# Down projection of a SwiGLU layer: float32r pairs made at each use, and scaled float16 pairs split once and kept in DRAM

## The chip, the cores and the metric

The kernel runs on one NeuronCore of a Trainium2 chip. TensorE (PE in the profile) multiplies, VectorE (DVE), ScalarE (ACT) and GpSimd (POOL) do the elementwise work, and SyncE (SP) issues nearly all transfers, in order, from one queue to 16 DMA engines. The metric is the device time of one execution in microseconds; of several runs the median is given.

## The reference

One layer of a hybrid backbone: 128 context tokens and 1024 latent tokens (1152 in all, nine blocks of 128), width 1024. A modulated RMS norm is followed by one input projection, which feeds a grouped-query attention (8 query heads, 2 key/value heads) and a bidirectional mLSTM (4 heads), side by side; an output projection merges them. Then comes the part that the change touches, the SwiGLU feed-forward layer with D_FF = 2816:

```python
def swiglu(h, w_gu, w_down):
    g, u = jnp.split(h @ w_gu, 2, axis=-1)
    return (jax.nn.silu(g) * u) @ w_down

    x = x + g1 * mix
    h2 = rmsnorm(x, norm2_w) * (1 + sc2) + sh2
    x = x + g2 * swiglu(h2, w_gu, w_down)
```

All inputs and outputs are float32. w_down has 2816 x 1024 elements: 22 row tiles of 128 rows.

## The kernel before

**Pairs.** No product is made in plain float32. A factor is split in a high part and the rest, and a product is the sum of three: high by high, high by rest, rest by high. In the input projection both parts are float16: the weights of a head are brought to a common power of two (class `Scaled`, L180: an absolute sum on ACT, four small DVE operations in `powers`, L159, a transpose and a one-row product in `power_scale`, L167), then split (`pairs`, L209). In the output projection and the feed-forward layer both parts are float32r: `load_piece` (L139) loads 512 KB of raw weights, ACT casts them (L152), and POOL, or DVE for each third piece, subtracts (L135). It has two raw buffers and five of each part. Each weight is loaded and split anew for each chunk.

**Chunks.** The feed-forward layer works on three chunks of three blocks (384 tokens). For a chunk, `gate_up` (L1275) makes, for a row tile f of 128 of the 2816 features, gate and up products of 24 matmuls each (384 columns), then tanh on ACT (L1298), two DVE operations (L1299, L1300) to the tile `tn`, and the pair `hl` by ACT (L1303) and POOL (L135). `down` (L1307) multiplies a group's rows by w_down, for each half of 512 output columns and each of the three blocks, through `three_blocks` (L1082; products L1090 to L1092), first block 0, then blocks 1 and 2. `add_gated` (L1076) multiplies the sum in PSUM by the gate row and adds it to x1. A group is 4 or 5 row tiles, five groups a chunk: gate/up of a group, then down of it, then the next. The last group of the last chunk has its own function, `down_last` (L1334; products L1356 to L1358), which finishes block by block and stores.

**Order.** The program is written as generators that yield after each unit of PE work. `weave` (L62) advances a side generator in proportion to the main one, `emit` runs one to its end; a scheduler then orders each engine's instructions by a simulated timeline, with the order of writing as priority (`hot` raises it). Beside the feed-forward work of a chunk runs the attention of the next chunk (50 units); then `attn_out` (L1178) merges it, and `norm2` (L1223) of the next chunk runs beside the last group's down projection. `finish` (L1319) normalises and stores the chunk before.

**The mLSTM stage.** `head_project` (L717) projects one head; beside it runs the scan of the head before (`head_mlstm`, L764) and, beside heads 0 to 2, `ada_rest` (L437), which loads the modulation weights (L443, three buffers, two loads ahead) and multiplies them (L318). The tiles b0 to b2 of the pool `hp` lie idle until attention.

**Banks.** In the feed-forward part PSUM has four banks of the kind `mm`, shared by gate/up, down, output projection and transposes; attention's scores and values have their own.

## Time and profile before

| | |
|---|---|
| median of 3 runs | 1627.77 us (1623.84 to 1633.02) |
| profiled execution, span | 1626.0 us (its time is given as the span alone) |
| mean granted TensorE clock | 0.972 |
| PE busy | 1517.4 us, 93% |
| DVE, ACT, POOL busy | 970.8, 732.5, 606.5 us |
| moved by DMA | 232.73 MB |

A line of the profile that groups instructions reads: line of the code, engine, operation, out<-in by the names of tiles, shapes, count | busy us in all, mean ns of one | idle us of the engine just before them, and what ended that idle time. A line of a table by stretches has the stretch, its length, then for PE, PE's weight loads, DVE, ACT and POOL the busy time and the count, the granted clock, the busy share of the DMA engines and GB/s. A line of the timeline has start, duration, engine, line and operation; matmuls are pipelined, so the distance between two starts, not the duration, tells the rate. A line of waits has who waited for whom, us in all, times, longest; a line of one tile's instructions has the count, then least, median and most ns.

### The profile page before, as it was taken

The page shows a single profiled execution, that of the slowest core. Times are in us where ns is not written, and L with a number is a line of the kernel's source. Part 1 is how long each engine was busy: PE and PEld are TensorE (multiplying, and loading weights), DVE is VectorE, ACT ScalarE, POOL GpSimd, SP SyncE. Part 2 cuts the span into 40 slices and gives each one's busy share as a digit, 9 for nine tenths or more (in the row PEclk, how much of TensorE's full clock was granted, in tenths as well). Part 3 has the DMA queues.
Part 4 walks back from the last instruction along what each step waited for, and adds up shares of the span by engine and source line. Part 5 has one row for each costly group of instructions (what it writes and reads, how often), then busy time and mean ns, then how long its engine had stood idle before and what let it go on. Part 6 is the DMA issues. An engine that isn't in the chain of part 4 may idle for free. (4 is left out here: it accounts for less than half of the span.)

```text
span 1626.0 us, 23528 instructions
## 1 busy us (share of the span) xinstructions
PE 1517.4 (93%) x8688; PEld 1258.8 (77%) x8688; DVE 970.8 (60%) x2059; ACT 732.5 (45%) x1251; POOL 606.5 (37%) x387
## 2 busy tenths in 40 slices
PE   5899899899879768999999999999999999999996
PEld 2745566575557557998989899898898989899995
DVE  3843364958987665467672646777674474432445
ACT  3744252434544554545643344565562453333332
POOL 0411020404344514443435354444344444545443
PEclk8999999999999878999999999999999999999998
DMA  9355352201156855767873546777684445545441
GB/s 357 94 165 130 101 147 58 84 21 46 41 198 147 195 107 112 168 168 174 187 184 112 149 141 219 187 184 173 156 183 128 134 142 170 152 126 149 130 142 66
DMA packets 386313, 232.73 MB, mean 143 GB/s; under 512 B 169910, under 2 KB 346502, under 8 KB 386198
## 3 DMA queue, kind: packets, MB, share of 16 engines
q1 hardware_dynamic: 384342, 228.04, 52.7%
q10 hardware_dynamic: 1856, 3.19, 0.6%
q8 instruction: 68, 1.11, 0.3%
q14 instruction: 47, 0.39, 0.1%
HBM read 181.16 MB, written 11.69 MB: 119 GB/s over the span
## 5 line engine op out<-in xcount | busy, mean ns | idle before, releaser
L135 POOL TENSOR_TENSOR wlo<-raw,whi 128x1024 fp32r<-128x1024 f32 x146 | 357.8, 2454 | 445.7 <-ACT whi L152 407.9
L152 ACT CAST whi<-raw 128x1024 fp32r<-128x1024 f32 x219 | 224.4, 1025 | 375.9 <-DMA raw<-in_w_gu_dram 137.8
L1272 PE MATMUL mm<-aTl,whi 128*128 128x384 f32 (+2 forms) x1088 | 364.7, 335 | 0.7 <-POOL aTl L135 0.7
L1273 PE MATMUL mm<-aTh,wlo 128*128 128x384 f32 (+2 forms) x1088 | 364.4, 335 | 0.0
L1271 PE MATMUL mm<-aTh,whi 128*128 128x384 f32 (+2 forms) x1088 | 363.4, 336 | 0.7 <-DVE tn L1299 0.7
L1272 PEld LDWEIGHTS mm<-aTl,whi 128*128 128x128 f32 x1088 | 205.9, 189 | 1.7 <-POOL aTl L135 0.9
L1271 PEld LDWEIGHTS mm<-aTh,whi 128*128 128x128 f32 x1088 | 205.4, 189 | 2.0 <-DVE tn L1299 1.3
L1273 PEld LDWEIGHTS mm<-aTh,wlo 128*128 128x128 f32 x1088 | 205.8, 189 | 0.1
L135 DVE TENSOR_TENSOR wlo<-raw,whi 128x1024 fp32r<-128x1024 f32 (+1 forms) x73 | 88.1, 1206 | 142.2 <-ACT whi L152 141.7
L1090 PE MATMUL mm<-whi,hl 128*128 128x512 f32 x372 | 145.8, 397 | 1.5 <-ACT hl L1303 1.4
L1091 PE MATMUL mm<-wlo,hl 128*128 128x512 f32 x372 | 146.9, 397 | 0.0
L1092 PE MATMUL mm<-whi,hl 128*128 128x512 f32 x372 | 144.3, 396 | 0.7 <-POOL hl L135 0.7
L1007 DVE SCALAR_TENSOR_TENSOR pl<-pr,st,ph 128x1152 f16<-128x1152 f32 (+1 forms) x72 | 107.8, 1498 | 39.4 <-ACT ph L1006 39.4
L488 PE MATMUL wi<-ipair,hT 128*128 128x384 f16 (+2 forms) x392 | 128.2, 327 | 2.8 <-ACT ipair L216 2.8
L489 PE MATMUL wi<-ipair,hT 128*128 128x384 f16 (+2 forms) x392 | 128.1, 327 | 0.0
L490 PE MATMUL wi<-ipair,hT 128*128 128x384 f16 (+2 forms) x392 | 127.1, 326 | 0.0
L135 POOL TENSOR_TENSOR hl<-tn,hl 128x384 fp32r<-128x384 f32 x66 | 84.2, 1276 | 105.0 <-ACT hl L1303 105.0
L1003 ACT ACTIVATE pr<-S,st 128x1152 f32<-128x1152 f32 (+1 forms) x72 | 81.1, 1127 | 89.1 <-DVE st L1002 86.1
L1299 DVE SCALAR_TENSOR_TENSOR tn<-tn,mm 128x384 f32<-128x384 f32 (+2 forms) x68 | 36.7, 540 | 137.9 <-PE mm L1273 97.5
L1080 DVE TENSOR_TENSOR x<-x,t 128x512 f32<-128x512 f32 x102 | 116.5, 1163 | 0.8
L1000 PE MATMUL S<-kst,qT 128*128 128x384 f32 (+1 forms) x400 | 88.3, 355 | 19.6 <-ACT pr L1003 19.2
L1002 DVE TENSOR_REDUCE st<-S 128x1 f32<-128x1152 f32 (+1 forms) x72 | 88.9, 1234 | 18.3 <-PE S L1000 17.8
(353 smaller groups left out, 2684.6 us busy)
## 6 DMA issues: line engine op xcount, KB each, us to landing
raw<-in_w_gu_dram SPq DMA_DIRECT2D x132, 512.0 KB
raw<-in_w_down_dram SPq DMA_DIRECT2D x60, 512.0 KB
a<-in_w_ada_dram SPq DMA_DIRECT2D x32, 512.0 KB
gl<-g_d SPq DMA_DIRECT2D x36, 256.0 KB
aw<-in_w_ada_dram SPq DMA_DIRECT2D x16, 512.0 KB
iraw<-in_w_in_dram SPq DMA_DIRECT2D x32, 256.0 KB
raw<-in_w_out_dram SPq DMA_DIRECT2D x15, 512.0 KB
x<-in_x_sample_dram SPq DMA_DIRECT2D x13, 512.0 KB
```

The source lines that it names most:

```text
L135: (dve if eng == "dve" else pool).tensor_tensor(out=out, in0=full, in1=hi, op=ALU.subtract)
L152: nc.scalar.copy(hi[:, :n], raw[:, :n])
L488: mm(ps[:, :n], ah, wh[:, k % 2, c0 : c0 + n], start=(k == 0), stop=False)
L489: mm(ps[:, :n], ah, wl[:, k % 2, c0 : c0 + n], start=False, stop=False)
L490: mm(ps[:, :n], al, wh[:, k % 2, c0 : c0 + n], start=False, stop=(k == KD - 1))
L1080: eng.tensor_tensor(out=x1[:, cs], in0=x1[:, cs], in1=t, op=ALU.add)
L1090: mm(ps, ah, wh[:, k % 2, :], start=(k == 0), stop=False)
L1091: mm(ps, ah, wl[:, k % 2, :], start=False, stop=False)
L1092: mm(ps, al, wh[:, k % 2, :], start=False, stop=(k == nk - 1))
L1271: mm(ps, wh[:, k, :], th[:, k, :], start=(k == 0), stop=False)
L1272: mm(ps, wh[:, k, :], tl[:, k, :], start=False, stop=False)
L1273: mm(ps, wl[:, k, :], th[:, k, :], start=False, stop=(k == KD - 1))
```

## The change

w_down is split once. `split_down`, run beside the projections of heads 0 and 1, takes each of the 22 row tiles: load 512 KB, an absolute sum per row on ACT, `powers` on DVE to get a power of two for each row, a scaled copy in float16 on ACT, the rest in float16 on DVE, and a store of the pair (512 KB) to a DRAM tile. The row scales stay in `wds`.

The down projection then loads float16 pairs straight into a ring of three tiles `wd` (each two row tiles by 512 columns, 512 KB), with no cast. The activations `tn` of a group are kept as float32, each with an absolute sum; when the group is whole, `rescale` finds one power of two for it (a maximum on DVE, a transpose, a maximum, `powers`, a one-row product, two small DVE operations), and each `tn` becomes a float16 pair with the row scale of w_down folded in (ACT, DVE). `tn` and pairs share 13 slots. `add_gated` undoes the scale.

Groups become 10 and 12 row tiles (10, 8 and 4 in the last chunk). Down of a group no longer follows its gate/up: it runs after the first four products of the next group; a chunk's last group is rescaled beside the first units of `attn_out` and multiplied after it, beside `norm2`. A half of the down projection now fills the three blocks' banks at once. `one1` and `wds` move to a pool that stays, and a scratch space of the program is made smaller.

```diff
-GROUPS = [(0, 4), (4, 4), (8, 4), (12, 5), (17, 5)]
-LAST = [(0, 5), (5, 5), (10, 4), (14, 4), (18, 4)]
+GROUPS = [(0, 10), (10, 12)]
+LAST = [(0, 10), (10, 8), (18, 4)]
+SLOTS = 13
...
+    wd_d = [drp.tile([P, 2, 2, 2, 512], F16, name=f"wd_d{j}") for j in range(NF // 2)]
...
+    def split_down():
+        def load(f):
+            t = hp.tile([P, 3, 1024], F32, name=nm("wdt"), tag=f"b{f % 3}")
+            dma(t[:, 0], w_down[f * P : (f + 1) * P, :])
+            return t
+        ahead = [load(0), load(1)]
+        yield
+        for f in range(NF):
+            t = ahead.pop(0)
+            if f + 2 < NF:
+                ahead.append(load(f + 2))
+            raw, v = t[:, 0], wds[:, f, :]
+            act(t[:, 2].bitcast(BF16)[:, 0:1024], raw, AF.Abs, accum_out=v[:, 0:1])
+            powers(v, P)
+            yield
+            o = t[:, 1].bitcast(F16).rearrange("p (n h x) -> p n h x", n=2, h=2)
+            raw = raw.rearrange("p (n x) -> p n x", n=2)
+            act(o[:, :, 0], raw, AF.Copy, scale=v[:, 2:3])
+            dve.scalar_tensor_tensor(out=o[:, :, 1], in0=raw, scalar=v[:, 2:3], in1=o[:, :, 0], op0=ALU.mult, op1=ALU.subtract)
+            dma(wd_d[f // 2][:, :, f % 2], o)
+            yield
...
-    weave(head_project(0, sts[0]), beside((gates, 0.6), (ada, 0.45)), 56, 56)
+    weave(head_project(0, sts[0]), beside((gates, 0.6), (ada, 0.45), (wd_steps, 0.4)), 56, 56)
...
-    weave(head_project(1, sts[1]), beside((scan, 1.15), (ada, 0.45)), 56, 56)
+    weave(head_project(1, sts[1]), beside((scan, 1.15), (ada, 0.45), (wd_steps, 0.45)), 56, 56)
+    emit(wd_steps)
...
-            hl = hlp.tile([P, 2, CT], F32R, name=nm("hl"), tag="hl", bufs=5)
-            ah, al = hl[:, 0], hl[:, 1]
-            nc.scalar.copy(ah, tn)
-            sub(al, tn, ah.bitcast(F32), "pool")
-            acts.append((ah, al))
+            jk = ft.tile([P, D], BF16, name=nm("jk"), tag="t2", bufs=3)
+            act(jk[:, 0:CT], tn, AF.Abs, scale=wds[:, f, 3:4], accum_out=g["st"][:, i : i + 1])
+            g["a"].append(tn)
+
+    def rescale(g):
+        f0, nf = g["f0"], g["nf"]
+        m = fp.tile([P, 16], F32, name=nm("gm"), tag="gm", bufs=2)
+        v = fp.tile([1, 4], F32, name=nm("gv"), tag="gv", bufs=2)
+        with hot(200):
+            dve.tensor_reduce(out=m[:, 0:1], in_=g["st"][:, 0:nf], axis=AX.X, op=ALU.max)
+            ps = bank()
+            transpose(ps[0:1, 0:P], m[:, 0:1])
+            dve.tensor_reduce(out=v[:, 0:1], in_=ps[0:1, 0:P], axis=AX.X, op=ALU.max)
+            powers(v, 1)
+        yield
+        with hot(200):
+            ps = bank()
+            mm(ps[:, 0:2], one1, v[:, 2:4], start=True, stop=True)
+            dve.tensor_copy(m[:, 1:3], ps[:, 0:2])
+            dve.tensor_scalar(out=m[:, 4 : 4 + nf], in0=wds[:, f0 : f0 + nf, 3], scalar1=m[:, 1:2], scalar2=None, op0=ALU.mult)
+        g["inv"] = m[:, 2:3]
+        for i, tn in enumerate(g["a"]):
+            hl = hlp.tile([P, 2, CT], F16, name=nm("hl"), tag="hl", bufs=SLOTS)
+            sc = m[:, 4 + i : 5 + i]
+            act(hl[:, 0], tn, AF.Copy, scale=sc)
+            dve.scalar_tensor_tensor(out=hl[:, 1], in0=tn, scalar=sc, in1=hl[:, 0], op0=ALU.mult, op1=ALU.subtract)
+            g["hl"].append(hl)
+        yield
...
+    def down_rows(g, j, n, tag="wd", bufs=3):
+        w = wp.tile([P, 2, 2, 512], F16, name=nm("wd"), tag=tag, bufs=bufs)
+        dma(w, wd_d[(g["f0"] + j) // 2][:, n])
+        return w
+
+    def down(c, a, g):
+        for n in range(2):
+            gate = gate_bc(1, c, n)
+            banks = [bank() for _ in range(CB)]
+            for j in range(0, g["nf"], 2):
+                w = down_rows(g, j, n)
+                for i, ps in enumerate(banks):
+                    down_products(ps, g, j, i, w)
+                    if j + 2 == g["nf"]:
+                        add_gated(a["x1"][i], ps, gate(c * CB + i), n, inv=g["inv"])
+                    yield 2
...
+    def groups(c, a, grps):
+        held = None
+        for g in grps:
+            ups = gate_up(a, g, 0, g["nf"])
+            if held is not None:
+                r = rescale(held)
+                next(r)
+                yield next(ups)
+                emit(r)
+                if g["nf"] > 4:
+                    for _ in range(3):
+                        yield next(ups)
+                    yield from down(c, a, held)
+                    yield from ups
...
-            emit(groups(c, cur, GROUPS[NG:-1]))
-            f0, nf = GROUPS[-1]
-            emit(gate_up(cur, f0, nf))
+            r = rescale(grps[-1])
+            next(r)
+            ao = attn_out(c + 1, nxt, oT, out_gates())
+            for _ in range(3):
+                next(ao)
+            emit(r)
+            emit(ao)
             n2 = chain(*[norm2(c + 1, nxt, i) for i in range(CB)])
-            weave(chain(down(c, cur, f0, nf, 0), down(c, cur, f0, nf, 1)), n2, 6 * nf, 8)
+            weave(down(c, cur, grps[-1]), n2, 6 * GROUPS[-1][1], 8)
```

`down_products` makes the same three products of a row tile and a block as L1090 to L1092, with float16 factors; `down_last` uses it with the tiles that `down_rows` loads.

112 lines of the change are left out of this document (49 added, 63 removed).

## The prediction

> **What bounds the kernel now.** I read first the page's shares, then stretches of the span in a table of busy time, then the waits of TensorE, and last the spacing of single matmuls in the timeline.
>
> ```profile
> PE 1517.4 (93%) x8688; PEld 1258.8 (77%) x8688; DVE 970.8 (60%) x2059; ACT 732.5 (45%) x1251; POOL 606.5 (37%) x387
> ```
> ```profile
> core 0: us, PE busy (x) PEld busy (x) DVE busy (x) ACT busy (x) POOL busy (x), PEclk, DMA share, GB/s
> 0.00:20.00 20.00, 13.12 (x69) 4.91 (x71) 5.78 (x29) 3.12 (x5) 0.76 (x6) 1.00 0.92 350
> ...
> 80.00:165.00 85.00, 82.10 (x554) 44.76 (x552) 35.14 (x115) 35.72 (x71) 9.72 (x12) 1.00 0.55 148
> 165.00:255.00 90.00, 87.50 (x632) 59.02 (x633) 43.41 (x154) 34.04 (x99) 13.15 (x21) 0.98 0.47 124
> ...
> 640.00:960.00 320.00, 315.50 (x1782) 290.60 (x1781) 181.42 (x262) 152.69 (x202) 135.97 (x66) 0.99 0.64 159
> 960.00:1310.00 350.00, 346.10 (x1916) 315.98 (x1915) 228.43 (x329) 175.55 (x233) 149.30 (x70) 1.00 0.65 168
> 1310.00:1606.00 296.00, 294.17 (x1544) 272.14 (x1543) 131.22 (x181) 101.28 (x134) 139.79 (x70) 1.00 0.47 139
> ```
>
> The last three rows are the feed-forward part, one row for each chunk of three blocks. TensorE (PE) stands idle there for 4.5 + 3.9 + 1.8 = 10.2 us of 966, at a granted clock of 0.99 to 1.00; DVE, ACT and POOL are at most 65%, 50% and 47% busy. So only what shortens TensorE's own stream, or those 10.2 us, can move the end there. The two rows from 80 to 255 are the first two mLSTM heads, where the change puts new work.
>
> A busy PE is not PE at its peak, so I take the rate from starts in unbroken runs: the down projection now (24 matmuls), the same width in float16 in the query projection (26), and a gate/up run (46).
>
> ```profile
> 1607.45 0.40 PE L1356 MATMUL mm<-whi,hl 128*128 128x512 f32 x1
> ...
> 1612.80 0.40 PE L1358 MATMUL mm<-whi,hl 128*128 128x512 f32 x1
> ```
> ```profile
> 445.79 0.38 PE L488 MATMUL mm<-ipair,hT 128*128 128x512 f16 x1
> ...
> 451.19 0.38 PE L490 MATMUL mm<-ipair,hT 128*128 128x512 f16 x1
> ```
> ```profile
> 860.10 0.34 PE L1271 MATMUL mm<-aTh,whi 128*128 128x384 f32 x1
> ...
> 867.90 0.34 PE L1271 MATMUL mm<-aTh,whi 128*128 128x384 f32 x1
> ```
>
> 5.35 us / 23 = 232.6 ns for one f32 matmul of 512 columns, 5.40 / 25 = 216.0 ns for one in f16, 7.80 / 45 = 173.3 ns in gate/up. The middle run has what the change makes: a pair of f16 halves on each side, three products, 512 columns.
>
> **Part 1, the product type.** The down projection has 396 triples:
>
> ```profile
> L1091 PE MATMUL mm<-wlo,hl 128*128 128x512 f32 x372 | 146.9, 397 | 0.0
> ...
> L1357 PE MATMUL mm<-wlo,hl 128*128 128x512 f32 x24 | 9.5, 394 | 0.0
> ```
>
> (372 + 24) x 3 = 1188 matmuls, before and after, each 16.6 ns closer to the next: **-19.7 us**, all on PE's own stream. 24 of these triples lie in the tail, where DVE finishes; they are 1.2 us of it.
>
> The Trainium skill, TensorE: Matmul & The Clock Gate, Back-to-back issue gap, gives one warm gap, N / 2.4 + 2.5 ns, that does not ask for the type: 215.8 ns at 512 columns. The f16 run agrees, the f32 run at 232.6 does not. By that rule the term would be zero; it is a rival below.
>
> **Part 2, work taken off the other engines.** The 60 full loads of raw w_down (and, by the code, 12 half ones) stay as 66 loads of pairs of 512 KB, the same bytes, but each loses its cast and its subtraction.
>
> ```profile
> raw<-in_w_down_dram SPq DMA_DIRECT2D x60, 512.0 KB
> ```
> ```profile
> L135 POOL TENSOR_TENSOR wlo<-raw,whi 128x1024 fp32r<-128x1024 f32 x132 | 330.9, 2511 | 413.0 <-ACT whi L152 375.2 <-issue 10.8 <-DVE t L1079 8.4
> L152 ACT CAST whi<-raw 128x1024 fp32r<-128x1024 f32 x195 | 204.5, 1049 | 326.3 <-DMA raw<-in_w_gu_dram 127.4 <-PE mm L1272 58.4 <-DMA raw<-in_w_down_dram 48.1
> ...
> L1080 DVE TENSOR_TENSOR x<-x,t 128x512 f32<-128x512 f32 x97 | 110.8, 1165 | 0.8
> L135 POOL TENSOR_TENSOR hl<-tn,hl 128x384 fp32r<-128x384 f32 x66 | 84.2, 1276 | 105.0 <-ACT hl L1303 105.0
> ...
> L1079 DVE TENSOR_TENSOR t<-mm,gl 128x512 f32<-128x512 f32 x88 | 58.5, 684 | 36.1 <-PE mm L1092 17.6 <-DMA gl<-g_d 10.4 <-PE mm L1358 6.7
> ...
> L1300 DVE TENSOR_TENSOR tn<-tn,mm 128x384 f32<-128x384 f32 x64 | 35.4, 553 | 1.6
> ...
> L1303 ACT CAST hl<-tn 128x384 fp32r<-128x384 f32 x66 | 33.7, 510 | 34.2 <-DVE tn L1300 34.0
> ```
>
> POOL loses the activations' subtraction (84.2) and, two pieces of three, some 40 x 2.5 us: about 185 us. ACT loses 60 x 1.049 us of casts and the half ones, 63 and a little, and gains 66 absolute sums, by the cast of a tile of that size (L1303) and a read of the accumulator (Part 4) 0.51 + 0.19 each: 46 us. DVE loses 48 of 90 gated additions, because 7 groups take the place of 15, at 0.684 + 1.165 us: 89 us; and gains the 66 activation subtractions, by L1300 about 37 us. PE covers all of it now and the sum takes **nothing** for it; without the cover it would be worth at most the 10.2 idle us.
>
> **Part 3, group boundaries.** PE's waits over these 966 us:
>
> ```profile
> PE S L1000 <- ACT pr L1003: 2.9, 2, 1.6
> PE mm L1090 <- ACT hl L1303: 1.4, 2, 1.1
> ...
> PE mm L1092 <- POOL hl L135: 0.7, 2, 0.5
> ```
>
> Waits for hl are of the old kind: projection, then at once the products that need its last row. Running a group's down products after four products of the next group takes these away, and a lighter DVE some of the others. Bounds 0 and -10.2; I take **-4**, nearer to the named waits (with their share of the pipeline's refill) than to the whole.
>
> The new rescale is late next. Its chain after a group's last row: ACT sum 0.51 + 0.19, eight small DVE operations of about 0.162, two small PE operations, then an ACT copy 0.51 and a DVE subtraction 0.55; queued behind its waits are, on PE, a transpose and a one-row product, and the whole down projection of the group.
>
> ```profile
> L1004 DVE RECIPROCAL st<-st 128x1 f32<-128x1 f32 x45 | 7.3, 162 | 41.8 <-ACT pr L1003 41.7
> ```
> ```profile
> L176 PE MATMUL mm<-pv,one 1*128 1x2 f32 x12 | 2.5, 273 | 1.7 <-DVE pv L165 1.7
> ...
> L114 PE MATMUL mm<-ident,isc 128*1 128x128 f32 x6 | 1.7, 289 | 4.5 <-DVE rv L125 4.5
> ```
>
> That is 0.70 + 1.30 + 0.56 + 1.06 = 3.6 us and its hand-overs. Between groups the cover is 4 x 24 x 0.1733 = 16.6 us; at the ends of the first two chunks it is the first output-projection block, 24 x 0.2326 = 5.6 us, and thin. If uncovered there: 7.2 us. PE's own 14 small operations cost between nothing and 7 x 0.56 = 3.9 us. Together 0 to 11; I take **+4**: half of the small operations, and a slip of 1 us at each thin place.
>
> Two more edits with the answer nothing. A group of twelve has one of the 13 activation slots to spare, so each pair waits for the tile before it to be given up: 1.06 us a row, while PE spends 9 x 0.216 = 1.9 us on it. And a down half now holds three of the four PSUM banks: the next half's first two blocks (12 x 0.216 = 2.6 us) start in the spare bank and in the one that was finished first, which covers an evacuation by DVE (0.684); uncovered, 12 halves would cost 8 us, and the range holds that.
>
> **Part 4, the split, 80 to 255 us.** For each of 22 row tiles: a load and a store of 512 KB, an absolute sum and a scaled copy on ACT, four small operations and a subtraction on DVE. The input weights go through the same operations in that stretch:
>
> ```profile
> L199 ACT ACTIVATE jk<-iraw x13: 1041/1057/1057, 87.9 to 307.0; 128x1024 bf16<-128x1024 f32 x13
> L199 ACT ACTIVATION_READ_ACCUMULATOR jk<-iraw x13: 185/186/188, 88.9 to 308.0; 128x1 f32 x13
> ...
> L216 ACT ACTIVATE ipair<-iraw,isc x8: 1146/1148/1165, 81.8 to 303.5; 128x1024 f16<-128x1024 f32 x8
> ...
> L217 DVE SCALAR_TENSOR_TENSOR ipair<-iraw,isc,ipair x8: 1272/1283/3143, 83.0 to 308.4; 128x1024 f16<-128x1024 f32 x8
> ```
>
> ACT: 22 x (1.057 + 0.186 + 1.148) = 52.6 us into 105 idle. DVE: 22 x (1.283 + 4 x 0.162) = 42.5 into 96 idle. The DMA engines: 23.1 MB, at the 350 GB/s of the first 20 us 66 us, onto 0.55 x 85 + 0.47 x 90 = 89 busy: 155 of 175. PE hides it while its stream never waits for a late a or ipair. SP runs its queue in order, and the 44 new issues (with a load that waits for an earlier store to land) stand among these:
>
> ```profile
> SPq L443 <- PE mm L318: 73.2, 20, 16.2
> ```
> ```profile
> PE mm L318 <- DMA a<-in_w_ada_dram: 4.4, 1, 4.4
> ```
>
> From 0 (all hidden, as nearly all loads are now) to 22 (five more such waits of 4.4): I take **+4**, one more.
>
> **Sum.** -19.7 - 4 + 4 + 4 = -15.7. The profiled execution's span is 1626.0, and no other time is given for it; so 1610.3. The median of the runs, 1627.77, stands 1.8 above that span: **1612 us**.
>
> **The rivals.** 0.5% is 8 us, about what a measurement of this kernel tells from no change.
>
> More: the boundary waits go entirely and split and rescale hide: -19.7 - 10.2 = -29.9, **1598**. For it: DVE and POOL much lighter. Against it: most of the 10.2 is attention's.
>
> No rate gain, f16 weights in the down stream still spaced at 232.6: -4 + 4 + 4, **1632**. Against it: the f16 run above, at 512 columns. This is what the Trainium skill's rule in Part 1 would come to.
>
> The split isn't hidden: ada's and the head weights' loads come late, five waits of 4.4: -19.7 - 4 + 4 + 22, **1630**. For it: DMA at 155 of 175, SP waits up to 16.2 us. Against it: one such wait now.
>
> Slower: the ring of three weight tiles. Before, five hi/lo slots lay between landing and use; now PE reads the landed tile itself, and its slot is refilled only after its 18 matmuls. A tile lasts 18 x 0.216 = 3.9 us, so two ahead cover 7.8. Landings on the chain of waits:
>
> ```profile
> 1352.81 6.72 DMA raw<-in_w_gu_dram
> ...
> 1365.53 5.80 DMA raw<-in_w_down_dram
> ...
> 1379.23 4.59 DMA raw<-in_w_down_dram
> ```
>
> These and about 0.4 of issue fit. Beyond 7.8 us a tile takes (latency + 3.9) / 3. There are 62 tiles on this path (22 + 22 + 18); the result is slower by 0.5% from (15.7 + 8.1) / 62 = 0.38 us a tile, so from a mean latency near 9 us. At 9.5 it is 4.47 a tile, +35: **1647**. For it: SP's order and attention's transposes. Against it: nothing landed that late here.
>
> **Chances.** Forecast 0.58 (own range 1602 to 1619), more 0.12, no rate gain 0.06, split not hidden 0.11, ring 0.13. Faster: forecast and more, 0.70. Same: 0.06 + 0.11 = 0.17. Slower 0.13. Range: down to 1598 less 3 for the spread of runs, 1595; up through 1630 and 1632 to 1633, which leaves out the ring.
>
> **What would show it.** Right: the down products at 216 ns from start to start, x396 for each of the three; PE's idle time from 640 to the end at or below 10 us; no PE wait on the wd tiles; 80 to 255 not longer by more than 5 us. Wrong: PE waits on DMA wd or on hl above 1 us each group (ring, rescale), a later first gate/up product than now (split), or a spacing near 232 ns.

## The result, and where the time went

The change makes the kernel slower. Its median is 1671.43 us (1668.08 to 1672.53, 4 runs) against 1625.80 us of the kernel before on the same chip (1617.71 to 1633.02, 4 runs): a ratio of 1.0278, with a 95 % interval from 1.0236 to 1.0320, some 45 us. The forecast was 1612 us, with a range up to 1633.

The profiled execution of the changed kernel has a span of 1669.1 us (its time is 1670.91), 43.1 us more than the span before. The page's shares:

```profile
PE 1526.5 (91%) x8709; PEld 1170.8 (70%) x8709; DVE 943.3 (57%) x2171; ACT 756.7 (45%) x1377; POOL 404.7 (24%) x273
```

POOL lost a third of its work, as forecast, and PE is busy 9 us longer although its products are quicker. The first gate/up product divides the span in two. A row of one line's instructions has the count, least, median and most ns, and then the first and the last start in us; first the kernel before, then the changed one:

```profile
L1271 PE MATMUL mm<-aTh,whi x70: 220/281/455, 622.1 to 667.0; 128*128 128x256 f32 x32, 128*128 128x128 f32 x32, 128*128 128x384 f32 x6
```
```profile
L1286 PE MATMUL mm<-aTh,whi x32: 279/283/364, 647.0 to 666.1; 128*128 128x256 f32 x32
```

Ahead of it 24.9 us are lost (622.1 to 647.0), behind it 18.2 (1003.9 to 1022.1), where the forecast had some 4 and -20. These are single traces: three later kernels that leave the feed-forward part as it was (`split_only`, `split_work`, `split_transfers`, below) took 999.5 to 1000.7 us behind the first product, so a difference of a few us between two traces says little.

**Ahead of it: the split.** The table by stretches of the changed kernel, with a stretch that the prediction did not look at (40 to 80 us, the preparation of the inputs); after it the row of the kernel before for that stretch:

```profile
core 0: us, PE busy (x) PEld busy (x) DVE busy (x) ACT busy (x) POOL busy (x), PEclk, DMA share, GB/s
40.00:80.00 40.00, 29.55 (x196) 21.91 (x196) 35.58 (x122) 34.82 (x74) 15.54 (x13) 0.84 0.73 234
80.00:165.00 85.00, 76.19 (x513) 41.75 (x511) 54.74 (x182) 58.72 (x104) 15.20 (x19) 0.98 0.87 281
165.00:255.00 90.00, 83.06 (x576) 54.46 (x575) 45.96 (x155) 45.90 (x112) 8.96 (x20) 0.94 0.67 180
665.00:985.00 320.00, 308.81 (x1764) 263.85 (x1763) 168.32 (x269) 156.52 (x235) 83.26 (x35) 0.98 0.60 149
985.00:1330.00 345.00, 333.62 (x1856) 282.15 (x1854) 191.16 (x300) 161.58 (x241) 77.02 (x31) 0.99 0.63 156
1330.00:1650.00 320.00, 311.28 (x1641) 244.10 (x1640) 119.22 (x210) 93.08 (x156) 65.92 (x28) 0.99 0.43 131
```
```profile
40.00:80.00 40.00, 34.96 (x262) 28.14 (x263) 36.67 (x120) 30.00 (x68) 18.79 (x18) 0.89 0.30 89
```

In the preparation of the inputs DVE was 92 % busy before, and ACT 75 %. PE did 262 matmuls there before and does 196 now. The rows of the split's tile show its work there:

```profile
L509 SPq DMA_DIRECT2D wdt<-in_w_down_dram x22: 327/340/1412, 47.8 to 188.1; - x22
L519 ACT ACTIVATE wdt<-wdt x22: 1040/1056/1087, 55.8 to 194.8; 128x1024 bf16<-128x1024 f32 x22
...
L525 DVE SCALAR_TENSOR_TENSOR wdt<-wdt,wds x22: 1262/1284/1697, 63.1 to 197.8; 128x1024 f16<-128x1024 f32 x22
```

It is written beside the projections of heads 0 and 1, which begin at 95 us here, but its loads begin at 47.8. They depend on nothing and the tiles lie idle, so nothing kept the scheduler from issuing them early.

**Behind it: the feed-forward part.** From the last three rows PE is idle 11.2 + 11.4 + 8.7 = 31.3 us of 985, before 10.2 of 966. PE's waits from 640 us to the end (who waits for whom: us in all, times, longest):

```profile
PE mm L115 <- DVE gm L1329: 15.9, 6, 3.9
PE po L1052 <- DMA phT<-ph: 3.3, 2, 2.1
...
PE mm L1355 <- DVE hl L1345: 1.2, 1, 1.2
```

The old waits for `hl` are gone, as forecast; but at six group ends the transpose in `rescale` waits for the group's maximum. The timeline of one of them, in the last chunk:

```profile
1459.00 0.33 PE L1288 MATMUL mm<-aTh,wlo 128*128 128x384 f32 x1
...
1460.61 0.62 ACT L1320 ACTIVATE jk<-tn,wds 128x384 bf16<-128x384 f32 x1 [0.33 <-DVE tn L1318]
1461.13 0.18 ACT L1320 ACTIVATION_READ_ACCUMULATOR jk<-tn,wds 128x1 f32 x1
1461.63 0.15 DVE L1329 TENSOR_REDUCE gm<-gst 128x1 f32<-128x10 f32 x1
...
1461.84 0.27 PE L115 MATMUL mm<-ident,gm 128*1 128x128 f32 x1 [2.51 <-DVE gm L1329]
...
1463.08 0.52 PE L1288 MATMUL mm<-aTh,wlo 128*128 128x384 f32 x1
...
1463.40 0.52 PE L1286 MATMUL mm<-aTh,whi 128*128 128x384 f32 x1
...
1465.95 0.34 PE L1288 MATMUL mm<-aTh,wlo 128*128 128x384 f32 x1
...
1466.13 0.34 PE L1286 MATMUL mm<-aTh,whi 128*128 128x384 f32 x1
```

The group's last gate/up product ends at 1459.33. PE's next instruction is the transpose, and it stands still for 2.51 us until the chain tanh, sum, maximum is through, though the next group's products, which were to cover it, stand ready behind it. From 1463.08 to 1465.95 the products then start 0.32 us apart instead of 0.17, and the table by stretches has a lower granted clock there, 0.83, between 1.00 and 1.00:

```profile
1450.00:1460.00 10.00, 9.33 (x54) 9.01 (x52) 1.66 (x3) 3.96 (x6) 4.80 (x2) 1.00 0.38 109
1460.00:1470.00 10.00, 8.16 (x38) 7.89 (x39) 3.54 (x11) 3.21 (x7) 1.10 (x1) 0.83 0.35 104
1470.00:1480.00 10.00, 10.00 (x58) 10.00 (x57) 9.42 (x13) 6.90 (x13) 3.71 (x2) 1.00 0.30 90
```

That costs another 10 x 0.146 = 1.5 us, so this place costs some 4 us. Not each place does. Of the six waits for `gm`, those of 2.51, 2.52, 2.52 and 3.86 us are followed by such a spell, those of 2.24 and 2.30 us are not; here is the stretch with the wait of 2.24:

```profile
1570.00:1580.00 10.00, 7.76 (x45) 7.17 (x44) 3.29 (x11) 4.22 (x7) 3.70 (x2) 1.00 0.36 105
```

Two more spells, at 773 and 1087 us, follow PE's waits for tiles of the attention. All six together cost 9.9 us, counted from the starts that lie wider apart in them.

**The spacings.** A down projection's block (24 starts), and a gate/up run (46 starts) of the changed kernel:

```profile
1350.73 0.38 PE L1353 MATMUL mm<-wd,hl 128*128 128x512 f16 x1
...
1355.69 0.38 PE L1355 MATMUL mm<-wd,hl 128*128 128x512 f16 x1
```
```profile
867.75 0.42 PE L1287 MATMUL mm<-aTl,whi 128*128 128x384 f32 x1
...
875.73 0.34 PE L1287 MATMUL mm<-aTl,whi 128*128 128x384 f32 x1
```

4.96 / 23 = 215.7 ns in the down projection, as forecast. 7.98 / 45 = 177.3 ns in gate/up, where the code is the same and it was 173.3. Over all gate/up starts of the two traces that are less than 250 ns apart, the means are 175.9 now and 173.5 ns before; with 3168 such products the difference is 7.7 us.

Added up behind the first product: -19.7 (type) + 21.1 (idle) + 7.7 (spacing) + 9.9 (half rate) = 19.0, against 18.2 in the two traces.

### The profile page after: what moved, and what is told of

Read it like the earlier page. It is cut to its first block, busy times and chain, and to the rows that moved or that the text cites. A ratio compares the mean times of both kernels' runs of the same rounds, so it can differ in the third digit from the quotient of the medians.

```text
span 1669.1 us, 23528 instructions
## 1 busy us (share of the span) xinstructions
PE 1526.5 (91%) x8709; PEld 1170.8 (70%) x8709; DVE 943.3 (57%) x2171; ACT 756.7 (45%) x1377; POOL 404.7 (24%) x273
## 5 line engine op out<-in xcount | busy, mean ns | idle before, releaser
L136 POOL TENSOR_TENSOR wlo<-raw,whi 128x1024 fp32r<-128x1024 f32 x98 | 240.9, 2459 | 708.6 <-ACT whi L153 649.3
L1286 PE MATMUL mm<-aTh,whi 128*128 128x384 f32 (+2 forms) x1088 | 368.6, 339 | 0.0
L153 ACT CAST whi<-raw 128x1024 fp32r<-128x1024 f32 x147 | 153.8, 1047 | 241.6 <-PE mm L1287 144.1
L1355 PE MATMUL mm<-wd,hl 128*128 128x512 f16 x396 | 150.1, 379 | 1.2 <-DVE hl L1345 1.2
L1354 PE MATMUL mm<-wd,hl 128*128 128x512 f16 x396 | 150.1, 379 | 0.0
L1353 PE MATMUL mm<-wd,hl 128*128 128x512 f16 x396 | 149.4, 379 | 0.4 <-DMA wd<-wd_d 0.4
L1034 ACT ACTIVATE ph<-pr,st 128x1152 f16<-128x1152 f32 (+1 forms) x72 | 83.2, 1158 | 24.8 <-ACT pr L1031 8.5
L136 DVE TENSOR_TENSOR wlo<-raw,whi 128x1024 fp32r<-128x1024 f32 x49 | 61.9, 1264 | 56.2 <-ACT whi L153 56.1
L1028 PEld LDWEIGHTS S<-kst,qT 128*128 128x128 f32 x400 | 74.0, 201 | 25.0 <-ACT pr L1031 23.1
```

Source lines behind the costliest of these rows:

```text
L136: (dve if eng == "dve" else pool).tensor_tensor(out=out, in0=full, in1=hi, op=ALU.subtract)
L153: nc.scalar.copy(hi[:, :n], raw[:, :n])
L1028: mm(S[:, n, 0:w], qT[:, h, :], kst[kv][:, t, c0 + n * w : c0 + (n + 1) * w], start=(t == 0), stop=(t == 1))
L1286: mm(ps, wh[:, k, :], th[:, k, :], start=(k == 0), stop=False)
L1353: mm(ps, ah, w[:, k, 0], start=(j + k == 0), stop=False)
L1354: mm(ps, ah, w[:, k, 1], start=False, stop=False)
```

## The experiments

Each ratio is to the kernel before, run beside it on the same chip, with its 95 % interval; 1 % is 16.2 us. "First product" is the start of the first gate/up product in the profiled run. In the kernels that have no ACT or DVE work of a split ahead of it, it lies between 617.2 and 622.1 us.

### The split by itself

`split_only` adds to the kernel before only this:

```diff
+    wds = cp.tile([P, NF, 4], F32, name="wds")
+    cp.tile([P, 40], F32, name="pad")
...
+    def split_down():     # as in the change
...
-    weave(head_project(0, sts[0]), beside((gates, 0.6), (ada, 0.45)), 56, 56)
+    weave(head_project(0, sts[0]), beside((gates, 0.6), (ada, 0.45), (wd_steps, 0.4)), 56, 56)
...
-    nc = _bacc.Bacc("TRN2", target_bir_lowering=False, num_devices=1)
+    nc = _bacc.Bacc("TRN2", target_bir_lowering=False, num_devices=1, dynamic_dma_scratch_size=1024)
```

> The kernel before, with the split of w_down alone: it is loaded, scaled, split and stored as in the change, but the feed-forward part doesn't read it and runs in float32 pairs as before. The weight tiles begin on a multiple of 256 bytes, as in the kernel before. Theory S (the split is issued far ahead of where it is written, into the preparation of the inputs, where ACT and DVE are full): the first head's projection starts 10 to 13 us later, the first gate/up product 20 to 25 us later, the time rises by 20 to 25 us, to about 1646 to 1651. The prediction's own step (the split finds idle time between 80 and 255 us): +4 us, about 1630. If the extra time of the change is all in the feed-forward part: within 3 us of before.

Measured: 1.0112 [1.0093, 1.0131], 18 us; first product 638.1 us. The split costs 18 us with nobody reading it, more than four times the +4 of the prediction and 2 us less than theory S gave.

Two kernels then take it apart. `split_work` keeps the operations, without transfers; `split_transfers` keeps the transfers, without operations:

```diff
-            t = ahead.pop(0)
-            if f + 2 < NF:
-                ahead.append(load(f + 2))
+            t = ts[f % 3]     # three tiles, filled with ones at the start
...
-            dma(wd_d[f // 2][:, :, f % 2], o)
```
```diff
-            act(t[:, 2].bitcast(BF16)[:, 0:1024], raw, AF.Abs, accum_out=v[:, 0:1])
-            powers(v, P)
...
-            act(o[:, :, 0], raw, AF.Copy, scale=v[:, 2:3])
-            dve.scalar_tensor_tensor(out=o[:, :, 1], in0=raw, scalar=v[:, 2:3], in1=o[:, :, 0], op0=ALU.mult, op1=ALU.subtract)
-            dma(wd_d[f // 2][:, :, f % 2], o)
+            dma(wd_d[f // 2][:, :, f % 2], t[:, 0].rearrange("p (n x) -> p n x", n=2))
```

> split_only with all 44 transfers of the split left out: ACT's and DVE's operations run on three tiles filled with ones, the rows of w_down are neither loaded nor stored. Theory W (what costs is the work, 53 us of ACT and 43 us of DVE in a stage without room): it costs what split_only costs, +16 to +20 us, about 1640. Theory Q (what costs is waiting in order: the loads come late because each waits for a store to land and stands in SP's queue behind other transfers, ACT waits at the load with all that is behind it, and DVE waits for ACT): most of the 18 us goes, +0 to +7 us, 1622 to 1629.

> split_only with the work of the split left out: each row tile of w_down is loaded and the same 512 KB are stored again as they are, through the same three tiles and the same queue; ACT and DVE do nothing for it. Theory W: +0 to +3 us, about 1625. Theory Q needs both, a late load and an engine that waits at it, so +0 to +5 us here; what is over that is the price of the transfers themselves for the loads of the other weights (the rival of the prediction that gave +8 us by late loads of the conditioning weights).

Measured: the work alone 1.0255 [1.0229, 1.0280], 41 us, first product 657.5; the transfers alone 1.0004 [0.9986, 1.0021], first product 618.3. Theory W's +16 to +20 us for the work alone is less than half of what was measured, but theory Q, that the cost is waiting in queues, falls, and with it the prediction's picture of DMA as the tight resource: the 40 to 80 us row of `split_transfers` has the DMA engines full and PE as busy as before (34.96):

```profile
40.00:80.00 40.00, 35.43 (x272) 29.37 (x273) 36.34 (x118) 32.17 (x71) 18.55 (x17) 0.90 1.02 353
```

The work costs more alone than with its loads. As I read it, that is because without loads nothing holds it back and the operations crowd together. All of it runs between 28 and 108 us; ACT is busy without a gap from 40 to 80, and PE is left with 98 matmuls of 262. The row of that stretch, the work's first and last start, and PE's longest wait from 40 to 95 us:

```profile
40.00:80.00 40.00, 21.22 (x98) 14.29 (x98) 36.84 (x127) 40.00 (x74) 7.25 (x6) 0.62 0.41 131
```
```profile
L515 ACT ACTIVATE wdt<-wdt x22: 1040/1082/1129, 27.8 to 94.1; 128x1024 bf16<-128x1024 f32 x22
...
L521 DVE SCALAR_TENSOR_TENSOR wdt<-wdt,wds x22: 1269/1279/2147, 34.1 to 107.6; 128x1024 f16<-128x1024 f32 x22
```
```profile
PE mm L115 <- DVE wds L163: 12.2, 3, 6.6
```

### The split, held back and spread

`split_gated` and `split_gated2` hold the first three loads of the changed kernel back; they differ in the tile that is copied from.

```diff
             t = hp.tile([P, 3, 1024], F32, name=nm("wdt"), tag=f"b{f % 3}")
+            if f < 3:
+                dve.tensor_copy(t[:, 0, 0:1], kall[:, 8, 0, 0:1])     # split_gated; split_gated2: kall[:, 7, 0, 0:1]
             dma(t[:, 0], w_down[f * P : (f + 1) * P, :])
```

> The changed kernel, with the first three loads of the split held back until the key and value projection has evacuated its last block (a one-column copy into each tile from that block's keys), so that nothing of the split runs during the preparation of the inputs. Theory S in its narrow form (the loss is in the preparation of the inputs): the 12.7 us there come back, the later 12 us stay, about 1658. Theory S in its wide form (ACT and DVE have no room for it in the head stage either): what is won ahead of the first head is lost again in the first heads, the first gate/up product stays within 5 us of 647.0, about 1668. The prediction's own step (no loss there): no change, 1671.

> The changed kernel, with the first three loads of the split held back by a one-column copy from the keys of the last token block, which the key and value projection writes at its end (split_gated copied from the cached keys, which are there at 27.6 us, and so held nothing back). Theory S in its narrow form (the loss is made in the preparation of the inputs, before the first head): the first head starts within 3 us of 82.4 us, as before the change, and 8 to 12 us come back, about 1660. Theory S in its wide form (the loss follows the split into the heads, because its operations stand ahead of others in ACT's and DVE's queues wherever it runs): the first head starts as before, but the first gate/up product stays at 640 to 647 us, within 4 us of 1668. If the input stage is late for another reason (the smaller scratch space, more transfers): the first head still starts at 92 to 95 us.

Measured: 1.0271 [1.0250, 1.0293] and 1.0290 [1.0272, 1.0307], against 1.0278 of the change: nothing. The first tells nothing, because its copies ran at 27.6 us, the keys of that index being cached ones. The second did hold the split back, to 88.1 us, the first head started on time (its first product at 81.7 us, 82.4 before), and the first product still came at 645.2: the wide form of theory S.

`ring_six` keeps that gate and puts two rows into each ring tile:

```diff
+            for k in range(2):
+                dma(t[:, k], w_down[(2 * q + k) * P : (2 * q + k + 1) * P, :])
...
+                o = t[:, (2, 0)[k]].bitcast(F16).rearrange("p (n h x) -> p n h x", n=2, h=2)
```

> The changed kernel, with the split held back until the keys of the last token block are there (as split_gated2, which took 1668), and with two row tiles in each of the three ring tiles, so that up to six rows are loaded ahead instead of three and a load waits for a store two steps older. Theory Q: ACT's wait for the split's loads, 31.5 us in split_gated2, falls under 10 us, the first gate/up product moves from 645 to 625 to 632 us, the time to 1648 to 1656. Theory W: the first gate/up product stays at 640 to 647 us, the time within 4 us of 1668.

Measured: 1.0257 [1.0233, 1.0280], first product 640.2. ACT's waits for the loads, `split_gated2` from 85 to 265 us and `ring_six` from 40 to 265:

```profile
ACT wdt L521 <- DMA wdt<-in_w_down_dram: 31.5, 15, 7.6
```
```profile
ACT wdt L523 <- DMA wdt<-in_w_down_dram: 7.5, 6, 3.3
```

24 us of waiting went, some 5 us of time came back (1.0290 to 1.0257; the intervals overlap).

### The rescale

`late_rescale` is the changed kernel with the transpose written later; its first steps also lose the raised priority.

```diff
-        with hot(200):
+        with nullcontext():     # around the maximum and the transpose
...
-                r = rescale(held)
-                next(r)
+                yield next(ups)
                 yield next(ups)
+                r = rescale(held)
+                next(r)
+                yield next(ups)
                 emit(r)
...
+                    d = down(c, a, held)     # in the last chunk
+                    for _ in range(3):
+                        yield next(d)
                     r = rescale(g)
                     next(r)
-                    d = down(c, a, held)
...
-            r = rescale(grps[-1])
-            next(r)
             ao = attn_out(c + 1, nxt, oT, out_gates())
             for _ in range(3):
                 next(ao)
+            r = rescale(grps[-1])
+            next(r)
+            for _ in range(3):
+                next(ao)
             emit(r)
```

> The changed kernel, with the transpose of each rescale issued two gate/up products (8.3 us of products) later, and that of the chunk's last group three blocks of the output projection later; the same for the product that spreads the scale. Theory R (the transpose stands in PE's queue ahead of the products that were to cover its chain, PE waits 2.4 to 4.0 us at each of six places, and the clock drops after each wait): the 15.9 us of wait before the transposes goes to under 2 us and the granted clock no longer drops there, the time falls by 18 to 25 us against the changed kernel, to 1646 to 1653. Rival (the same waits move to the float16 products, which then wait for the rescaled tiles): the time stays within 5 us of 1671. The prediction's step (rescale costs 4 us in all): a fall of at most 4 us, 1667.

Measured: 1.0143 [1.0119, 1.0166] against 1.0278: 22 us less, by the two intervals between some 14 and 30; theory R. The wait for `gm` is gone; part of it has moved on to the tiles themselves, and three spells at half rate are left behind waits of 2.0 to 2.6 us for them, where theory R had none. PE's waits from 640 us on in `late_rescale`:

```profile
PE mm L1353 <- ACT hl L1344: 6.5, 6, 2.4
PE mm L1353 <- DVE tn L1317: 4.3, 2, 2.6
```

### The address of the weight tiles

The change puts `wds` (352 bytes of each partition) and `one1` (512) ahead of the pool of the weight tiles, 864 bytes or 3 x 256 + 96, and shrinks a scratch space. No run prints where the pool begins, so I tell the moves alone. `pad_before` moves the weight tiles of the kernel before by 96 bytes, and with them the pools behind them on that side of the memory; `pad64_before` moves them by 64; `after_aligned` adds 160 bytes in the changed kernel, so that 864 becomes 4 x 256.

```diff
     vsc = cp.tile([P, 4], F32, name="vsc")
+    pad = cp.tile([P, 24], F32, name="pad")     # pad64_before: 16; after_aligned: 40
+    dve.memset(pad, 0.0)
```

> The kernel before, with one unused tile of 96 bytes per partition, so that the weight tiles begin at 96 modulo 128 as in the changed kernel, not on a multiple of 256. Theory A (the address of the weight tiles sets the spacing of the float32 gate/up products): the spacing goes from 173.4 to about 175.9 ns, over 3168 products +7 to +8 us, about 1633. Rival (the spacing rises because of other work, the float16 tiles or the transfers): spacing stays at 173.4 ns, time within 2 us of before.

> The kernel before, with one unused tile of 64 bytes per partition instead of pad_before's 96, so that the weight tiles begin at a multiple of 64 that is not one of 128. If a start on a multiple of 64 bytes is enough: spacing 173.4 to 173.9 ns, time within 3 us of before. If it has to be one of 128 or more: about 176 ns as in pad_before, +7 to +8 us.

> The changed kernel, with an unused tile of 160 bytes per partition, so that the weight tiles begin on a multiple of 256 bytes again. Theory A: the float32 gate/up products are spaced 173.4 to 173.8 ns apart again instead of 176.5, over 3168 of them a fall of 8 to 9 us, to about 1662. Rival (in the changed kernel the float16 tiles or the larger traffic set the spacing, whatever the address): spacing stays at 176 ns, time within 2 us of 1671.

Measured: `pad_before` 1.0048 [1.0029, 1.0066], 7.8 us, mean gate/up spacing 175.9 ns (again of the starts less than 250 ns apart); `pad64_before` 1.0020 [1.0006, 1.0035], spacing 173.5; `after_aligned` 1.0244 [1.0221, 1.0266], 5.5 us less than the change, spacing 173.5. The first and last start in a run of 46 in `pad_before` are 7.92 us apart, 176.0 ns each:

```profile
855.12 0.34 PE L1273 MATMUL mm<-aTh,whi 128*128 128x384 f32 x1
...
863.04 0.34 PE L1273 MATMUL mm<-aTh,whi 128*128 128x384 f32 x1
```

Theory A holds for the spacing: a move by 96 bytes raises it, one by 64 does not. In time it is less sharp. `pad64_before`, with the old spacing, is still 3.2 us slower than the kernel before, which the spacing does not explain, and the 5.5 us of `after_aligned` are not clear of the noise of the two ratios.

### All repairs together, and other places for the split

`split_in_ffn` does the split in the first chunk, in `gate_up`, with tiles of the rings `raw` and `wd`; `combined` adds the late rescale and the moved tiles.

```diff
+            if a.get("split"):
+                split_row(f)     # raw = wp.tile(..., tag="raw", bufs=2); pair = wp.tile(..., tag="wd", bufs=3)
```

> The changed kernel, with the same split done in the first chunk of the feed-forward part, one row tile ahead of each pair of gate/up products, in tiles of the feed-forward part's own rings; nothing of it is left ahead of the feed-forward part. There ACT was busy 27 us and DVE 30 to 34 us of each 50, and the split adds 2.4 us of ACT and 2 us of DVE per 8.3 us of products. Theory S: the first gate/up product starts at 620 to 625 us again, the feed-forward part grows by at most 5 us, the time falls by 16 to 25 us against the changed kernel, to 1646 to 1655. Rival (the split costs the same wherever it is put): within 5 us of 1671. The prediction's step (the split cost 4 us where it was): a fall of at most 4 us.

> The changed kernel with all three repairs: the split in the first chunk of the feed-forward part, the rescale's transpose behind two gate/up products, the weight tiles on a multiple of 256 bytes. If S, R and A are separate costs: 1671 less 18 to 25, 22 and 8, so 1616 to 1623, between 0 and 7 us faster than before (the product type's 16.6 to 19.7 us less what the rescale still costs, some 10 us). If one of them only moves into another wait: 1630 or more.

Measured: 1.0962 [1.0939, 1.0985] and 1.0795 [1.0779, 1.0811]. The head stage was free again (first products 620.2 and 619.5), but behind it `split_in_ffn` took 1159.6 us, against 1022.1 of the change. The row tiles of the split take turns in a ring of two with the gate/up weights and stay there far longer than those; PE's longest waits from 600 to 1000 us are for the gate/up weights:

```profile
PE mm L1274 <- ACT whi L153: 31.9, 18, 4.6
PE mm L1276 <- POOL wlo L136: 26.3, 17, 2.3
```

The two differ by 1.67 %, 27 us, by the repairs of rescale and address: 22 and 5.5 by themselves.

The forecast of 1646 to 1655 us, and that of 1616 to 1623 for all repairs together, were far off: this place for the split, with this ring, costs more than the one it replaces.

`combined2` is `ring_six`, with the tiles moved and the rescale late, at a chunk's end behind two units instead of three, and its scaling of the held tiles raised to `hot(200)`.

> The changed kernel with three repairs: the split as in ring_six, the weight tiles on a multiple of 256 bytes, and the rescale's transpose behind two gate/up products (at a chunk's end behind two units of the output projection, and the scaling of the held tiles ahead of other work of ACT and DVE). If theories Q, R and A hold: 1668 less 12 to 20, less 22 and less 8 to 11, so 1615 to 1626, between 0.4 % faster and 0.3 % slower than before. If Q falls: 1634 to 1640.

Measured: 1.0034 [1.0020, 1.0047]. What is left of the loss stands ahead of the first product, at 640.8; behind it are 1628.8 - 640.8 = 988.0 us, 15.9 less than in the trace before the change and 11.5 to 12.7 less than in the three traces named above. PE's idle time is 12.8 us of 949:

```profile
659.00:1608.00 949.00, 936.17 (x5248) 775.07 (x5247) 472.64 (x776) 412.91 (x630) 222.31 (x93) 1.00 0.56 151
```

`combined3` spreads the same work over all four heads, each pair's loads held back by a block of the running head; `combined4` in addition makes the scales of two row tiles at once.

```diff
-            if q < 3:
-                dve.tensor_copy(t[:, 0:2, 0:1], kall[:, 7:8, 0, 0:2].rearrange("p a b -> p b a"))
+            dve.tensor_copy(t[:, 0:2, 0], gate[0][:, 0:2])     # kt of the last block projected
...
-    weave(head_project(0, sts[0]), beside((gates, 0.6), (ada, 0.45), (wd_steps, 0.4)), 56, 56)
+    weave(head_project(0, sts[0]), beside((gates, 0.6), (ada, 0.45), (wd_steps, 0.17)), 56, 56)     # and heads 1, 2, 3
```

> combined2, with the loads of each pair of row tiles held back until the keys of a block of the running head are there, and the steps of the split written beside all four heads' projections instead of the first two: the same work of ACT and DVE over 85 to 400 us instead of 95 to 209 us. Theory D (the loss comes from how densely the split stands between other operations in ACT's and DVE's order): the first gate/up product moves from 640.8 to 622 to 630 us, the time from 1626.7 to 1608 to 1616, about 0.5 % faster than before. Theory N (each of its operations costs the same wherever it stands in the heads): the first gate/up product stays at 637 to 643 us, the time at 1623 to 1630.

> combined3, with the four small DVE operations that make a row tile's scale done for two row tiles at once, 44 of 88 operations of 0.14 us fewer, 6.2 us of DVE. Theory D: within 2 us of combined3. Theory N: 2 to 6 us less than combined3, in the proportion that the split's work costs.

Measured: 1.0062 [1.0042, 1.0082], first product 643.4, with the work from 94.6 to 307 us; and 1.0031 [1.0014, 1.0048], first product 634.8. Spreading gained nothing, so theory D falls (the trace of `combined3` is of the slowest of its 12 executions, 1640.7 us against a median of 1633.6). Taking 6.2 us of DVE's work away gained about 5 us (the intervals just overlap), as theory N has it.

`combined5` and `combined6` go back to the first chunk, with the ring `wd`, which they share with the float16 pairs, in place of the gate/up weights' ring, and with ACT's queue for the transfers; in `combined6` a row tile's first operation also waits for the activations of the row tile before.

```diff
+        raw = wp.tile([P, 1024], F32, name=nm("wdr"), tag="wd", bufs=3)
+        dve.tensor_copy(raw[:, 0:2], held)
+        nc.scalar.dma_start(raw, w_down[f * P : (f + 1) * P, :])
...
+        dve.tensor_copy(o.rearrange("p n h x -> p (n h x)")[:, 0:2], held)     # combined6
```

> combined2's rescale and weight tiles, with the split in the first chunk of the feed-forward part, between the gate and the up product of each row tile; unlike in split_in_ffn its tiles are those of the float16 pairs' ring, not the two raw tiles of the gate/up weights, and its transfers are issued on ACT's queue, not SP's. If split_in_ffn's 106 us came from the shared ring and queue (PE's longest waits there were for the gate/up weights' casts, 31.9 us, and subtractions, 26.3 us): the first gate/up product starts at 617 to 624 us, the feed-forward part takes 988 to 993 us, the time is 1606 to 1616, 0.4 to 1.0 % faster than before. If the 53 us of ACT and 43 us of DVE cost wherever they stand: some 15 to 20 us in the first chunk, 1625 or more.

> combined5, with the first operation of the split on each row tile held back by a two-column copy from the activations of the row tile before, so that its load, issued a period of about 8 us earlier, has landed. If the loss in combined5's first chunk is ACT standing at late loads: ACT's wait for them falls from 40.6 us to under 10, the time from 1647.6 to 1608 to 1622. If it is the work of the split: within 6 us of 1647.

Measured: 1.0157 [1.0140, 1.0173] and 1.0175 [1.0152, 1.0198], with first products at 618.4 and 620.6. Without the gate/up weights' ring and SP's queue the time is 6 % below that of `combined`, but the split still costs some 38 us behind the first product (1027.4 and 1026.0 against 988.0 in `combined2`, which has the same repairs). ACT's wait of 40.6 us for the split's loads in `combined5`

```profile
ACT wdo L517 <- DMA wdr<-in_w_down_dram: 40.6, 15, 5.5
```

falls to 0.5 us in `combined6` (one more wait of 10.8 us, of an operation of the attention, names such a load), and the time is the same: not the late loads. In its first chunk, 620.6 to 960 us, PE is idle for 25.8 us at a granted clock of 0.93; in that of `combined2`, 640.8 to 982, for 6.9 at 0.99. So 19 of the 38 us are PE standing still, and the lower clock is worth about the rest (0.06 of 340 us is 20). PE's two longest waits in `combined6` from 610 to 960 us name DVE:

```profile
PE mm L115 <- DVE gm L1334: 6.4, 1, 6.4
PE mm L1359 <- DVE wds L165: 5.9, 1, 5.9
```

No kernel with the split was faster than the kernel before.

## Why the prediction was wrong, by its steps

**Part 1, the product type: right.** 215.7 ns a start, 396 triples, -19.7 us. `combined2`, with 12 to 16 us less behind the first product, shows that most of this gain reaches the end once the rest is out of its way. The rival of no rate gain fell. The Trainium skill, TensorE: Matmul & The Clock Gate, Back-to-back issue gap, gives N / 2.4 + 2.5 ns, 215.8 at 512 columns, for a single matmul on its own, which the prediction did not say, and about 131 ns for a stream. The float16 streams here agree with the first figure; no run here shows the second, and the float32 streams, at 232.6, agree with neither.

**Part 2, the work taken off: right in size.** POOL went from 606.5 to 404.7 us. That it is worth nothing, as forecast, fits the sum behind the first product, but no run takes it by itself.

**Part 3, the rescale: the step that failed is "between groups the cover is 4 x 24 x 0.1733 = 16.6 us".** The four products stand behind the transpose in PE's queue; they cover what comes after it, not the wait for the maximum. The prediction even listed the transpose as "queued behind its waits", and did not ask what stands behind the transpose. It took +4 for the chain, with an upper bound of 11; the six waits alone came to 15.9 us, and four of them brought a spell at half rate of some 1.5 us, for which the prediction had no term. That makes some 22 us, and moving the transpose gained 22 (`late_rescale`); as new waits arose there, that the two agree so well is in part luck. The old waits for `hl` went, as forecast.

**Part 4, the split: the step that failed is "52.6 us into 105 idle" and "42.5 into 96 idle", taken as cover.** The term of +4 was too small by 14 to 21 us (18 us in `split_only`, 24.9 in the changed kernel's profile); that its bounds of 0 to 22 came near is luck, for the reason did not hold. It priced the split by late transfers; these cost nothing by themselves (`split_transfers`), and in the changed kernel PE waits 6.4 us for `a` ahead of 640 us, where the prediction had read 4.4:

```profile
PE mm L320 <- DMA a<-in_w_ada_dram: 6.4, 2, 5.6
```

The operations cost, wherever they were put: in the preparation of the inputs, in two heads, in four heads, in the feed-forward part. And the stretch was wrong: the prediction took 80 to 255 us from where the generator is written, while the split began at 47.8.

Idle time of ACT and DVE was no cover. The row of ACT's longest wait in the kernel before, from 85 to 265 us, shows what that idle time is:

```profile
ACT kt L728 <- PE wi L490: 44.1, 8, 10.6
```

ACT is idle there because it waits for a sum; when the sum comes, PE in turn soon needs the bank or the operand that ACT and DVE make of it. That an operation of 1.1 to 1.3 us which stands at that moment in the queue delays PE is how I read it; no run shows it instruction by instruction. Shown is that the cost comes with the operations of ACT and DVE and not with the transfers, and that no place tried hid it. Its size is not fixed by the amount of work: the same operations cost 18 us in `split_only`, 41 without their loads, and some 38 in the first chunk. Which instruction pays in the first chunk of `combined6` stays open, and so does whether the ring shared with the float16 pairs plays a part.

**Not in the prediction: the address of the weight tiles.** The move of `one1` and `wds` and the smaller scratch space were read and given no price. The move of the weight tiles costs up to 7.8 us (`pad_before`); 2.43 ns on each of 3168 products make 7.7, but a move that keeps the spacing cost 3.2 too, so the share of the spacing is not settled.

**The rivals.** That the split isn't hidden was priced at 1630, by waits for late loads; the price of the split was right within some us, by luck, the mechanism was not. The ring of three weight tiles, the only case on the slower side, did not happen: in the changed kernel PE waits 0.4 us for `wd` in all.

```profile
L1353 PE MATMUL mm<-wd,hl 128*128 128x512 f16 x396 | 149.4, 379 | 0.4 <-DMA wd<-wd_d 0.4
```

**The sum as measured.** By the ratios, in us of 1622: `combined2` +5.5; rescale +21.9; address +5.5 (in the changed kernel) or +7.8 (in the kernel before); gate and ring of the split +3.4. That is 36 to 39 of 45. The rest may be what `combined2` does to the rescale beyond `late_rescale`, which was not run by itself, or the noise of the ratios: that of the changed kernel alone is uncertain by 7 us either way.

## What to carry to other kernels

Ask of each wait that a change adds what stands behind it in the same engine's queue, and issue a product that depends on a long chain behind the products that are to cover the chain. Idle time in a table by stretches is room only for work that nobody waits behind; where an engine is idle because it stands in a loop with the bounding one, do not count that time as cover before a run with the added work alone has shown it. When a change moves a pool of matmul weights, move it by a multiple of 64 bytes, and compare the spacing of untouched products as a control.

## What the runs showed of the hardware that I had not expected

**Address and rate.** float32 gate/up matmuls of 384 columns start 175.9 ns apart instead of 173.5 when the tiles of their weights are moved by 96 bytes; moved by 64, they keep 173.5. Here "weights" is the operand held in the array, the second one in a row of the profile. Products that stream from the moved tiles hardly changed: those of the down projection in `pad_before`, `mm<-whi,hl`, are 233.2 ns apart instead of 232.5, and the float16 ones are 216.0 apart in the changed kernel and in `after_aligned`. But these have 512 columns, and so do the output projection's, `mm<-whi,mx`, whose held operand lies in a moved pool too and which are 228.0 apart instead of 227.3. Whether the operand's part or the number of columns decides, the runs do not tell.

**Half rate after a short stop.** In the timeline above the last product ends at 1459.33, PE stands for 2.51 us, works on from 1461.84, and the spacing doubles only from about 1462.8 on, 3.4 us after that end, for about 3.2 us. The Trainium skill, TensorE: Matmul & The Clock Gate, Part 1, tells of an idle window of about 3.4 us. The length agrees; but here PE had already worked again for about a quarter of it, so a stop of 2.5 us was enough. It is no threshold: in `late_rescale` a stop of 2.0 us is followed by a spell at half rate, in `after_aligned` those of 2.24 and 2.30 us are, and one of 2.52 us is not.

**DVE beside POOL.** In the timeline of `late_rescale`, the same DVE subtraction takes 2.01 us while POOL subtracts, and 0.61 after; an addition of 0.69 us elsewhere takes 2.85. Of the 66 subtractions of this kernel, the 56 that run with POOL's subtractions nowhere beside them take 0.60 to 0.62 us.

```profile
955.52 0.69 DVE L1111 TENSOR_TENSOR x<-x,t 128x512 f32<-128x512 f32 x1
...
957.86 5.04 POOL L136 TENSOR_TENSOR wlo<-raw,whi 128x1024 fp32r<-128x1024 f32 x2 [15.02 <-ACT whi L153]
...
958.66 2.01 DVE L1345 SCALAR_TENSOR_TENSOR hl<-tn,gm,hl 128x384 f16<-128x384 f32 x1
...
960.60 2.85 DVE L1111 TENSOR_TENSOR x<-x,t 128x512 f32<-128x512 f32 x1
...
963.37 0.61 DVE L1345 SCALAR_TENSOR_TENSOR hl<-tn,gm,hl 128x384 f16<-128x384 f32 x1
```

A chain priced by a DVE row's mean can so be three to four times as long where POOL runs beside it.
